# Softmax denominators added up on GpSimd instead of VectorE, in a two-block network of one core

## The chip, the core and the metric

The kernel runs on one core of one Trainium2 chip. The metric is device time in microseconds (us) of one execution. The core's engines each run their own queue of instructions in order: TensorE (PE in the rows; PEld is its weight load), VectorE (DVE), ScalarE (ACT), GpSimd (POOL) and SyncE (SP), which here issues all DMAs. Engines wait for each other through semaphores.

## What is computed

The network is a block with two hybrid layers (retention, neighbourhood attention and grouped-query attention in parallel, merged by gates), followed by a second block of feed-forward layers and two mixers. 256 tokens, a context of 256 more, width 1024, all in float32. The change touches the softmax of the two attentions. Cut to that:

```python
def attend(q, k, v):
    s = jnp.einsum('btkgd,bskd->bkgts', q, k).astype(jnp.float32) * (q.shape[-1] ** -0.5)
    p = jax.nn.softmax(s, axis=-1)
    return jnp.einsum('bkgts,bskd->btkgd', p, v)
...
        s_all = jnp.concatenate([s.reshape(s.shape[:5] + (n_loc,)), s_ctx], axis=-1)
        p = jax.nn.softmax(s_all, axis=-1)
        p_loc = p[..., :n_loc].reshape(s.shape)
        p_ctx = p[..., n_loc:]
        return jnp.einsum('bhrjqwk,brwjkhd->brjqhd', p_loc, vb) + jnp.einsum('bhrjql,blhd->brjqhd', p_ctx, vc)
...
    for layer in range(DEPTH):
        x, y = hybrid_layer(x, y, ..., need_ctx=layer < DEPTH - 1)
```

Layer 0 gives results for the 256 tokens and for the context (512 queries); layer 1 for the tokens alone (256 queries).

## The kernel before

Everything is kept transposed: the 128 partitions hold keys (or channels), the free dimension holds queries. A product is made in several fp32r passes of a high and a low part (`mm3`, `split`, `pair`), so a weight is first cast to a high part by ScalarE (`wh`) and its rest is subtracted by VectorE (`wl`).

One call of `scores` handles one head. Its scores lie in tiles of 128 keys: `s_loc` holds the scores against the two token tiles side by side, `cs` those against the two context tiles (two tiles of 512 queries in layer 0, one tile with both halves in layer 1). Then, in this order of the data: VectorE takes the maximum over the key tiles into `m`; GpSimd's `partition_all_reduce` takes the maximum of `m` over the 128 partitions and leaves it in all of them (`mx`, line 801); VectorE subtracts `mx` from every score tile; ScalarE takes the exponential (line 815); `pair` splits it into high and low parts; TensorE multiplies them with the values (`av`). For the denominator, VectorE adds the tiles of exponentials over the key tiles into `d` (lines 820 to 825: one add of the two context tiles, and one for each token tile), and a second `partition_all_reduce` sums `d` over the partitions (`den`, line 826). `den` is not needed by `av`; `pair_sums` (line 866) needs it, once both heads of a pair are multiplied, and the pair's result `o` is needed by the merge of its branch (`t_merge`).

The adds are there where `both` is set: in the four head pairs of neighbourhood attention of layer 0 (tiles named L0n), the four pairs of grouped-query attention of layer 0 (L0g) and the four pairs of neighbourhood attention of layer 1 (L1n). That is 24 calls of `scores` and 72 adds. Grouped-query attention of layer 1 (L1g) gets its denominators from TensorE. In neighbourhood attention a token key tile reaches only 160 of the 256 token queries (`REACH`), so the two adds of `s_loc` are 128x160; in L0g they are 128x256; the first add is 128x512 in layer 0 and 128x256 in layer 1.

The program does not write its instructions in the order in which they run. Every call goes to a recorder (`_Recorder.record`, which issues all of them from line 343, so nearly every row carries that line); `schedule` then plays the whole program through a list scheduler, with a cost for each operation from `cost` and a due time, and `issue` writes each engine's instructions in the planned order. So the costs in `cost` set the order on every engine. TensorE's queue mixes the attention of one branch with the merge of another: the L0m rows are merge products, L0gk keys and values, `ada_ps` modulation.

Of the kernel before, what the change touches and what calls it, by code (L numbers as in the profile page):

```python
# [10 lines left out]
ALU = mybir.AluOpType  # L11
# [4 lines left out]
T = 256  # L16
# [87 lines left out]
class _Recorder:  # L104
# [19 lines left out]
    def cost(self, eng, method, out, ins, kw):  # L124
        n = 1
        for e in out.shape[1:]:
            n *= e
        psum = any(i.space == bass.MemoryType.PSUM for i in ins) or out.space == bass.MemoryType.PSUM
        if eng == "tensor":
            rhs = ins[-1]  # L130
            n = 1
            for e in rhs.shape[1:]:
                n *= e
            d = max(n, 64) / 2400.0 * (4 if rhs.dtype == F32 and method == "matmul" else 1) + 0.002
            return d * 0.31 if out.shape[0] == 32 else d
        if eng == "scalar":
            return (n + (61 if psum else 112)) / 1200.0 + 0.093 * (len(ins) - 1)
        if eng == "vector":
            per = {"reciprocal": 6.0, "tensor_tensor_scan": 2.0}.get(method, 1.0)
            if method == "tensor_scalar" and not psum:  # L140
                per = 0.5
            if method == "tensor_reduce":
                n = 1
                for e in ins[0].shape[1:]:
                    n *= e
            return (66 + per * n) / 960.0 + (0.06 if method == "scalar_tensor_tensor" and len(ins) == 3 else 0)
        if eng == "gpsimd":
            return 0.38 + 7.5 * n / 1200.0 if method == "partition_all_reduce" else 0.09 + n / 1200.0
        b = 4
        for e in out.shape:  # L150
            b *= e
        return b / 360e3
# [193 lines left out]
class _K:  # L346
# [410 lines left out]
    def scores(self, qk, nq, bias, scale, both):  # L757

        nc = self.nc

        def passes(out, ks, n):
            for i, (k, q) in enumerate(qk):
                self.mm(out, lhsT=k[:, ks], rhs=q[:, n], start=i == 0, stop=i == len(qk) - 1)

        v2 = self.v2
        sx = self.ps()
        reach, w = (FULL, T) if bias is None else (REACH, NR)  # L770
        for kt in range(2):
            passes(sx[:, w * kt : w * kt + w], slice(P * kt, P * kt + P), reach[kt])
        cs = []
        m = self.f()
        if nq == T:
            s = self.ps()
            for kt in range(2):
                ks = slice(T + P * kt, T + P * kt + P)
                passes(s[:, 256 * kt : 256 * kt + 256], ks, FULL[0])
            c = self.f()  # L780
            nc.scalar.copy(c, s)
            self.tt(m[:, :T], c[:, :T], c[:, T:], ALU.max)
            cs.append(c)
        else:
            for kt in range(2):
                s = self.ps()
                ks = slice(T + P * kt, T + P * kt + P)
                passes(s, ks, slice(0, nq))
                c = self.f()
                nc.scalar.copy(c, s)  # L790
                cs.append(c)
            self.tt(m, cs[0], cs[1], ALU.max)
        s_loc = self.f()
        if bias is None:
            nc.scalar.copy(s_loc, sx)
        else:
            self.tt(s_loc[:, : 2 * w], sx[:, : 2 * w], bias, ALU.add)
        for kt, c in enumerate(reach):
            self.tt(m[:, c], m[:, c], s_loc[:, w * kt : w * kt + w], ALU.max)
        mx = self.f()  # L800
        nc.gpsimd.partition_all_reduce(mx[:, :nq], m[:, :nq], channels=P, reduce_op=RED.max)
        mb = mx[:, :T].unsqueeze(1).to_broadcast([P, 2, T])
        out = []
        for i, e in enumerate([s_loc] + cs):
            n = 2 * w if i == 0 else T2
            if i == 0 and bias is not None:
                ml = mx[:, :T]
                ml = bass.AP(ml.tensor, ml.offset, [list(ml.ap[0]), [T - NR, 2], [1, NR]])
                ev = e[:, :n].rearrange("p (a b) -> p a b", a=2)
                self.tt(ev, ev, ml, ALU.subtract)  # L810
            elif i == 0 or nq == T:
                self.tt(v2(e), v2(e), mb, ALU.subtract)
            else:
                self.tt(e, e, mx, ALU.subtract)
            self.act(e[:, :n], e[:, :n], AF.Exp, scale=scale)
            out.append(self.pair(e, n))
        if not both:
            return out, None
        den, d = self.f(), self.f()
        if nq == T:  # L820
            self.tt(d[:, :T], cs[0][:, :T], cs[0][:, T:], ALU.add)
        else:
            self.tt(d, cs[0], cs[1], ALU.add)
        for kt, c in enumerate(reach):
            self.tt(d[:, c], d[:, c], s_loc[:, w * kt : w * kt + w], ALU.add)
        nc.gpsimd.partition_all_reduce(den[:, :nq], d[:, :nq], channels=P, reduce_op=RED.add)
        return out, den

# [412 lines left out]
    def v2(self, t):  # L1241
        return t.rearrange("p (a b) -> p a b", a=2)
# [446 lines left out]
```

## Time and profile before

| | |
|---|---|
| median of 3 runs | 1872.78 us (1872.41 to 1873.35) |
| the profiled execution's own time | 1871.89 us |
| its span in the trace | 1870.1 us |
| TensorE busy | 1831.5 us (98%), 11392 matmuls |
| VectorE busy | 1489.0 us (80%) |
| ScalarE busy | 1108.9 us (59%) |
| GpSimd busy | 206.7 us (11%), 152 instructions |
| share of TensorE in the chain that ended last | 90% |

The span leaves out 1.8 us around the program. A busy share is an average over the whole program; attention of layer 0 lies between about 160 and 500 us of the span, neighbourhood attention of layer 1 between about 780 and 890 us. A row of the trace gives a start, a duration and, in brackets, how long the engine sat idle before it and which instruction ended that.

### The profile page before, as it was taken

The page shows a single profiled execution, that of the slowest core. Times are in us where ns is not written, and L with a number is a line of the kernel's source. Part 1 is how long each engine was busy: PE and PEld are TensorE (multiplying, and loading weights), DVE is VectorE, ACT ScalarE, POOL GpSimd, SP SyncE. Part 2 cuts the span into 40 slices and gives each one's busy share as a digit, 9 for nine tenths or more (in the row PEclk, how much of TensorE's full clock was granted, in tenths as well). Part 3 has the DMA queues.
Part 4 walks back from the last instruction along what each step waited for, and adds up shares of the span by engine and source line. Part 5 has one row for each costly group of instructions (what it writes and reads, how often), then busy time and mean ns, then how long its engine had stood idle before and what let it go on. Part 6 is the DMA issues. An engine that isn't in the chain of part 4 may idle for free.

```text
span 1870.1 us, 29383 instructions
## 1 busy us (share of the span) xinstructions
PE 1831.5 (98%) x11392; PEld 1618.8 (87%) x11392; DVE 1489.0 (80%) x2389; ACT 1108.9 (59%) x1884; POOL 206.7 (11%) x152
## 2 busy tenths in 40 slices
PE   6999999999999999999999999999999999999998
PEld 4888787777889989999998889988888888988887
DVE  7778978699947699998789877898767876788764
ACT  4655555666545596766566556875546554756543
POOL 0133422042200021232000000000000010000000
PEclk9999999999999999999999999999999999999999
DMA  9432353334344323435656566265555555545552
GB/s 314 134 97 87 113 160 113 113 90 153 99 154 125 90 69 90 143 109 150 194 169 225 180 199 218 78 217 196 192 189 187 192 186 197 192 158 181 186 195 92
DMA packets 336235, 291.17 MB, mean 156 GB/s; under 512 B 9184, under 2 KB 325728, under 8 KB 336096
## 3 DMA queue, kind: packets, MB, share of 16 engines
q1 hardware_dynamic: 336096, 289.30, 49.0%
q8 instruction: 89, 1.46, 0.3%
q14 instruction: 50, 0.41, 0.1%
HBM read 288.22 MB, written 1.05 MB: 155 GB/s over the span
## 4 chain that ended last, share of the span: by engine, by line
PE 90%; DVE 6%; ACT 2%; issue 1%; DMA 0%; POOL 0%; SPq 0%; DVEq 0%; POOLq 0%; ACTq 0%
PE fb_ps L343 13%; PE L0m_ps L343 8%; PE f_ps L343 7%; PE fa_ps L343 7%; PE L1m_ps L343 5%; PE L0n_ps L343 5%; PE L1n_ps L343 4%; PE L0r_ps L343 4%; PE L1r_ps L343 4%; PE fb1b_ps L343 3%; PE f0b_ps L343 3%; PE fb0b_ps L343 3%; PE fa1b_ps L343 3%; PE mix_ps L343 3%; PE L0g_ps L343 3%; PE L0out_ps L343 3%
## 5 line engine op out<-in xcount | busy, mean ns | idle before, releaser
L343 PE MATMUL fb_ps<-fb_r,fb_wh 128*128 128x512 f32 x704 | 176.6, 393 | 0.0
L343 PEld LDWEIGHTS fb_ps<-fb_r,fb_wh 128*128 128x128 f32 x704 | 126.7, 189 | 22.8
L343 ACT CAST fb_wh<-fb_raw 128x1024 fp32r<-128x1024 f32 x88 | 92.1, 1049 | 87.1 <-PE fb_ps L343 58.3
L343 DVE TENSOR_TENSOR fb_wl<-fb_raw,fb_wh 128x1024 fp32r<-128x1024 f32 x88 | 107.6, 1223 | 35.7 <-ACT fb_wh L343 35.4
L343 PE MATMUL L0m_ps<-L0in_r,L0m_wh 128*128 128x512 f32 x384 | 121.2, 394 | 0.0
L343 PEld LDWEIGHTS fb_ps<-fb_r,fb_wl 128*128 128x128 f32 x704 | 96.0, 190 | 6.8
L343 PE MATMUL fb_ps<-fb_r,fb_wl 128*128 128x256 f32 x704 | 98.1, 282 | 0.0
L343 PE MATMUL f_ps<-f_r,f_wh 128*128 128x512 f32 x352 | 88.7, 393 | 0.0
L343 PE MATMUL fa_ps<-fa_r,fa_wh 128*128 128x512 f32 x352 | 88.4, 393 | 0.0
L343 PEld LDWEIGHTS L0m_ps<-L0in_r,L0m_wh 128*128 128x128 f32 x384 | 72.3, 190 | 16.4 <-issue 0.8
L343 POOL MEMSET mix_r<- 128x128 f32 (+1 forms) x36 | 7.4, 238 | 640.9 <-DVE fa_r L343 457.9
L343 DVE TENSOR_TENSOR L0g_r<-L0g_r,L0g_r 128x512 f32<-128x512 f32 (+3 forms) x116 | 71.5, 663 | 6.4 <-ACT L0g_r L343 3.8
L343 PE MATMUL L0m_ps<-L0in_r,L0m_wl 128*128 128x512 f32 x192 | 75.3, 393 | 0.0
L343 ACT ACT_TABLE_LOAD x56 | 71.8, 1283 | 4.4 <-PE L0out_ps L343 1.4
L343 ACT CAST fa_wh<-fa_raw 128x1024 fp32r<-128x1024 f32 x44 | 46.1, 1049 | 47.5 <-PE fa_ps L343 29.9
L343 PEld LDWEIGHTS fa_ps<-fa_r,fa_wh 128*128 128x128 f32 x352 | 63.4, 189 | 11.4
L343 PEld LDWEIGHTS f_ps<-f_r,f_wh 128*128 128x128 f32 x352 | 63.4, 189 | 11.4
L343 DVE TENSOR_TENSOR fa_wl<-fa_raw,fa_wh 128x1024 fp32r<-128x1024 f32 x44 | 53.8, 1223 | 24.3 <-ACT fa_wh L343 18.0
L343 PE MATMUL L1m_ps<-L0out_r,L1m_wh 128*128 128x256 f32 x384 | 71.9, 283 | 0.0
L343 ACT CAST f_wh<-f_raw 128x1024 fp32r<-128x1024 f32 x44 | 46.1, 1049 | 42.4 <-PE f_ps L343 24.6
L343 DVE TENSOR_TENSOR fb_r<-fb_r,fb_r 128x512 f32<-128x512 f32 (+2 forms) x132 | 65.7, 509 | 2.3 <-ACT fb_r L343 1.3
L343 ACT CAST L0m_wh<-L0m_raw 128x1024 fp32r<-128x1024 f32 (+1 forms) x48 | 40.1, 837 | 44.3 <-PE L0m_ps L343 25.9
(509 smaller groups left out, 5464.8 us busy)
## 6 DMA issues: line engine op xcount, KB each, us to landing
fb_raw<-in_ffn_w_in_dram SPq DMA_DIRECT2D x44, 1024.0 KB, 5.4
f_raw<-in_ffn_w_in_dram SPq DMA_DIRECT2D x22, 1024.0 KB, 5.2
fa_raw<-in_ffn_w_in_dram SPq DMA_DIRECT2D x22, 1024.0 KB, 5.2
ada_raw<-in_ada_w_dram SPq DMA_DIRECT2D x32, 512.0 KB, 4.8
L0m_raw<-in_w_in_dram SPq DMA_DIRECT2D x24, 512.0 KB, 3.8
L1m_raw<-in_w_in_dram SPq DMA_DIRECT2D x24, 512.0 KB, 4.2
L0in_raw<-in_ada_w_dram SPq DMA_DIRECT2D x32, 256.0 KB, 6.0
f0b_raw<-in_ffn_w_out_dram SPq DMA_DIRECT2D x8, 1024.0 KB, 5.5
```

What stands on the lines that cost most here:

```text
L343: getattr(getattr(self.real, eng), method)(*a, **k)
```

## The change

The three adds of the denominator are issued to GpSimd (the argument `nc.gpsimd` of `tt`) and not to VectorE. The maxima, the subtractions and both `partition_all_reduce` stay where they were. The planner's cost for GpSimd changes with it: an operation other than `partition_all_reduce` was 0.09 + n/1200 us for n elements a partition, and is now 0.1 us plus n/960 for each input (half of that for a memset, which has none). Since the planner sets the order, instructions move on the other engines too.

```diff
         if eng == "gpsimd":
-            return 0.38 + 7.5 * n / 1200.0 if method == "partition_all_reduce" else 0.09 + n / 1200.0
+            if method == "partition_all_reduce":
+                return 0.38 + 7.5 * n / 1200.0
+            return 0.1 + n * (len(ins) or 0.5) / 960.0
...
         if nq == T:
-            self.tt(d[:, :T], cs[0][:, :T], cs[0][:, T:], ALU.add)
+            self.tt(d[:, :T], cs[0][:, :T], cs[0][:, T:], ALU.add, nc.gpsimd)
         else:
-            self.tt(d, cs[0], cs[1], ALU.add)
+            self.tt(d, cs[0], cs[1], ALU.add, nc.gpsimd)
         for kt, c in enumerate(reach):
-            self.tt(d[:, c], d[:, c], s_loc[:, w * kt : w * kt + w], ALU.add)
+            self.tt(d[:, c], d[:, c], s_loc[:, w * kt : w * kt + w], ALU.add, nc.gpsimd)
         nc.gpsimd.partition_all_reduce(den[:, :nq], d[:, :nq], channels=P, reduce_op=RED.add)
```

VectorE's queue has 72 instructions fewer. GpSimd's has the 72 adds more, and 58 others that stand nowhere in the source: an `ISA` row without a tile is what the compiled program calls a reload of the engine's library, and the builder puts one wherever an add follows a `partition_all_reduce` or the other way round. Memsets need none. The program before has one such reload, ahead of its first `partition_all_reduce`; the changed one has 59: 20 of the new ones among the L0n heads, 20 among L0g, 18 among L1n.

GpSimd's queue of the kernel before, at the first two head pairs of L0n (an `ISA` row with tiles is a `partition_all_reduce`; 385 and 409 are the maxima of pair 0, 392 and 416 its denominators, 437 and 456 the maxima of pair 1):

```order
L343 ISA L0n_r_385<-L0n_r_379 128x512
L343 ISA L0n_r_409<-L0n_r_403 128x512
L343 MEMSET L0n_r_517 64x512
L343 ISA L0n_r_392<-L0n_r_393 128x512
L343 MEMSET L0n_r_518 64x512
L343 ISA L0n_r_416<-L0n_r_417 128x512
L343 ISA L0n_r_437<-L0n_r_431 128x512
L343 ISA L0n_r_456<-L0n_r_450 128x512
```

The same place of the changed kernel, from behind maximum 409 on:

```order
L345 ISA
L345 TENSOR_TENSOR L0n_r_393<-L0n_r_381,L0n_r_383 128x512
L345 MEMSET L0n_r_517 64x512
L345 TENSOR_TENSOR L0n_r_393<-L0n_r_393,L0n_r_384 128x160 x2
L345 ISA
L345 ISA L0n_r_392<-L0n_r_393 128x512
L345 ISA
L345 TENSOR_TENSOR L0n_r_417<-L0n_r_405,L0n_r_407 128x512
L345 MEMSET L0n_r_518 64x512
L345 TENSOR_TENSOR L0n_r_417<-L0n_r_417,L0n_r_408 128x160
L345 ISA
L345 ISA L0n_r_437<-L0n_r_431 128x512
```

Ahead of maximum 437 there now stand four reloads, five adds and one denominator (416 comes later); behind it, ahead of maximum 456, come two more reloads and one add.

GpSimd's queue of the kernel before at the last pair of L0g (948 and 970 are its maxima, 955 and 977 its denominators; behind it follow memsets of layer 1):

```order
L343 ISA L0g_r_948<-L0g_r_942 128x512
L343 ISA L0g_r_970<-L0g_r_964 128x512
L343 ISA L0g_r_955<-L0g_r_956 128x512
L343 ISA L0g_r_977<-L0g_r_978 128x512
L343 MEMSET L1gk_r_1305 128x2x64
```

And of the changed kernel:

```order
L345 ISA L0g_r_948<-L0g_r_942 128x512
L345 ISA L0g_r_970<-L0g_r_964 128x512
L345 ISA
L345 TENSOR_TENSOR L0g_r_956<-L0g_r_944,L0g_r_946 128x512
L345 TENSOR_TENSOR L0g_r_956<-L0g_r_956,L0g_r_947 128x256 x2
L345 ISA
L345 ISA L0g_r_955<-L0g_r_956 128x512
L345 ISA
L345 TENSOR_TENSOR L0g_r_978<-L0g_r_966,L0g_r_968 128x512
L345 TENSOR_TENSOR L0g_r_978<-L0g_r_978,L0g_r_969 128x256 x2
L345 ISA
L345 ISA L0g_r_977<-L0g_r_978 128x512
```

Four reloads and six adds now stand between the last maximum and the last denominator.

## Rows read from the trace of the kernel before

**Rows 1.** The page: span, engines' busy us, engines' shares of the chain that ended last.

```profile
span 1870.1 us, 29383 instructions
...
PE 1831.5 (98%) x11392; PEld 1618.8 (87%) x11392; DVE 1489.0 (80%) x2389; ACT 1108.9 (59%) x1884; POOL 206.7 (11%) x152
...
PE 90%; DVE 6%; ACT 2%; issue 1%; DMA 0%; POOL 0%; SPq 0%; DVEq 0%; POOLq 0%; ACTq 0%
```

**Rows 2.** Waits of TensorE: us in total, times, longest.

```profile
PE L0g_ps L343 <- DVE L0g_r L343: 2.5, 3, 1.5
PE L0n_ps L343 <- ACT L0n_r L343: 2.4, 1, 2.4
PE L0g_ps L343 <- ACT L0g_r L343: 1.9, 2, 1.4
```

**Rows 3.** VectorE's groups, 160 to 330 us: busy us, mean ns.

```profile
L343 DVE TENSOR_TENSOR L0n_r<-L0n_r,L0n_r 128x512 f32<-128x512 f32 x36 | 29.6, 840 | 0.7 <-ACT L0n_r L343 0.7
...
L343 DVE TENSOR_TENSOR L0n_r<-L0n_r,L0n_r 128x160 f32<-128x160 f32 x32 | 11.8, 371 | 0.3
```

**Rows 4.** VectorE's groups, 780 to 890 us, the same columns.

```profile
L343 DVE TENSOR_TENSOR L1n_r<-L1n_r 128x256 f32<-128x256 f32 x16 | 6.9, 438 | 0.3 <-ACT L1n_r L343 0.2
```

**Rows 5.** GpSimd's instructions from line 343: duration ns min/median/max, first and last start.

```profile
L343 POOL MEMSET L0n_r<- x8: 518/522/547, 100.6 to 224.3; 64x512 f32 x8
...
L343 POOLq MODIFY_POOL_CONFIG  x2: 11/11/11, 0.8 to 0.8; - x2
```

**Rows 6.** GpSimd's timeline, 330 to 520 us: start, us, what, idle before.

```profile
357.25 1.78 POOL L343 PARTITION_ALL_REDUCE L0g_r<-L0g_r  x1 [28.73 <-DVE L0g_r L343]
...
485.05 9.20 POOL L343 PARTITION_ALL_REDUCE L0g_r<-L0g_r  x2 [6.08 <-DVE L0g_r L343]
```

**Rows 7.** ScalarE's loads of function tables, in the page: busy us, mean ns.

```profile
L343 ACT ACT_TABLE_LOAD x56 | 71.8, 1283 | 4.4 <-PE L0out_ps L343 1.4
```

**Rows 8.** DMA issues: times, KB of each, median us from issue to landing.

```profile
fb_raw<-in_ffn_w_in_dram SPq DMA_DIRECT2D x44, 1024.0 KB, 5.4
...
L0r_raw<-in_w_in_dram SPq DMA_DIRECT2D x2, 1024.0 KB, 7.5
...
L0n_b<-in_na_dram SPq DMA_DIRECT2D x8, 160.0 KB, 3.4
```

**Rows 9.** GpSimd's timeline, 170 to 330 us.

```profile
178.43 2.08 POOL L343 PARTITION_ALL_REDUCE L0n_r<-L0n_r  x1 [3.92 <-DVE L0n_r L343]
...
191.61 5.28 POOL L343 PARTITION_ALL_REDUCE L0n_r<-L0n_r  x2 [5.10 <-DVE L0n_r L343]
198.77 2.08 POOL L343 PARTITION_ALL_REDUCE L0n_r<-L0n_r  x1 [1.88 <-DVE L0n_r L343]
...
303.14 3.23 POOL L343 PARTITION_ALL_REDUCE L0n_r<-L0n_r  x1 [1.77 <-DVE L0n_r L343]
```

**Rows 10.** TensorE's timeline, 205 to 214 us: products with the values, pair 1 of L0n.

```profile
205.24 0.50 PE L343 MATMUL L0n_ps<-L0n_r,L0n_r 128*128 128x512 f32 x1 [2.44 <-ACT L0n_r L343]
...
212.65 1.48 PE L343 MATMUL L0n_ps<-L0n_r,L0n_r 128*128 128x512 f32 x8
```

**Rows 11.** TensorE's timeline, 489 to 505 us: first wait of the merge of L0g.

```profile
504.63 0.50 PE L343 MATMUL L0m_ps<-L0g_r,L0m_wh 128*128 128x512 f32 x1 [0.77 <-DVE L0g_r L343]
```

**Rows 12.** GpSimd's timeline, 745 to 900 us: first and last of L1n.

```profile
791.51 1.06 POOL L343 PARTITION_ALL_REDUCE L1n_r<-L1n_r  x1 [19.44 <-DVE L1n_r L343]
...
884.51 3.58 POOL L343 PARTITION_ALL_REDUCE L1n_r<-L1n_r  x2 [10.08 <-DVE L1n_r L343]
```

**Rows 13.** TensorE's timeline, 908 to 911 us: the merge's first product with L1n.

```profile
909.48 0.40 PE L343 MATMUL L1m_ps<-L1n_r,L1m_wh 128*128 128x256 f32 x2
```

**Rows 14.** Stretch, length, busy us (instructions) by engine, granted clock, DMA share, GB/s.

```profile
378.71:385.54 6.83, 6.04 (x15) 4.62 (x16) 6.83 (x11) 5.42 (x10) 4.61 (x2) 0.50 0.52 144
...
200.00:210.00 10.00, 7.37 (x34) 5.52 (x33) 10.00 (x14) 6.96 (x13) 0.85 (x1) 1.00 0.66 186
```

**Rows 15.** VectorE's timeline, 170 to 210 us: an add beside a reduction.

```profile
191.99 2.04 DVE L343 TENSOR_TENSOR L0n_r<-L0n_r,L0n_r 128x160 f32<-128x160 f32 x1
```

## The prediction

> **What bounds the kernel now.** I read the page first, then the waits of TensorE, then the timelines of GpSimd and TensorE beside each other in the three stages where the moved adds stand. TensorE is busy 1831.5 of 1870.1 us and makes 90% of the chain that ended last [rows 1]: matmuls are the bound nearly everywhere, and the time can fall only by what TensorE waits. In the two attention stages of layer 0 these waits are 2.5 + 2.4 + 1.9 us, and 0.8 us more at the merge behind them [rows 2, 11]: 7.6 us, of which 3.3 us were ended by VectorE. After the short waits in L0g the granted clock was 0.50 of full speed for 6.83 us (the lower of the two levels, 1.2 GHz), which costs 3.4 us; around the single wait of 2.44 us in L0n it stayed 1.00 [rows 10, 14]. So relief of VectorE is worth at most 7.6 + 3.4 = 11 us. There is far more room the other way: TensorE's queue is in order, and a product with the values that waits for its exponentials holds up all that follows it.
>
> **What the change removes.** 72 adds leave VectorE. By its groups a 128x512 add takes 0.84 us, a 128x160 one 0.37, a 128x256 one 0.44 [rows 3, 4]. L0n: 8 heads x (0.84 + 2 x 0.37) = 12.6 us; L0g: 8 x (0.84 + 2 x 0.44) = 13.8; L1n: 8 x (0.44 + 2 x 0.37) = 9.4. That is 36 us of VectorE's time, but nearly all of it lies beside busy TensorE. I credit the 3.3 us of waits that VectorE ended.
>
> **What it adds to GpSimd: the adds.** No row shows an add on GpSimd. From below, a memset of 512 elements, which reads nothing, takes 0.52 us [rows 5]; from above, an undisturbed reduction over the partitions of 512 elements takes 1.78 us [rows 6]. I take the middle, 1.15 us, since an add reads two tiles but crosses no partitions, and in proportion 0.6 us for 256 and 0.4 us for 160 elements.
>
> **What it adds to GpSimd: the reloads.** The queue now holds 58 reloads of the engine's library, between adds and reductions. The one of before is two records of 11 ns at 0.8 us of the span, 85 us ahead of the first reduction [rows 5], so the trace doesn't show how long the engine can't work after one. The bounds: from below those records, or 1.28 us, what ScalarE takes to load a table of functions [rows 7]; from above 7.5 us, the slowest landing of a DMA in the rows, 1 MB; a piece of 160 KB lands after 3.4 us, the most frequent load of 1 MB after 5.4 us [rows 8]. A reload is a program that is fetched while the engine stands still, so I put it with the transfers and take **R = 5.4 us**.
>
> The Trainium skill, GPSIMD Engine Reference, section 2.1, speaks against this change: the first call of a freshly loaded kernel "additionally pays an IRAM-load of approximately 6 µs", with no instruction in the profile that shows it. No run here shows that yet; the records of 11 ns agree with its being invisible. With 6 us the sum below would come to about 2010 us, an estimate from that page.
>
> **Where the reloads lie: L0n.** The second maximum of pair 0 ends at 180.5 us and that of pair 1 at 200.85 [rows 9]. Between them the changed queue has six reloads; the six adds of pair 0, 2 x (1.15 + 0.4 + 0.4) = 3.9 us; two memsets, 1.0; one denominator, 3.2 [rows 9]; two maxima at 2.1, 4.2. That is 12.3 + 6R = 44.7 us, so the maximum ends at 225.2 us, 24.4 us late. The first head's product stood waiting when it began 8.35 us after its maximum (191.61 + 5.28 to 205.24); the second head's began 11.8 us after its own, at 212.65 [rows 9, 10], so 3.4 us are slack. TensorE waits **21 us** more there. In pairs 2 and 3 GpSimd catches up in its idle time before it, and I take 3 us (0 to 6) for the last maximum.
>
> **L0g.** Here GpSimd has no rest. Its work from the first maximum on: 8 maxima at 2.1 and 8 denominators at 3.2 us, 42.4; adds 8 x (1.15 + 1.2) = 18.8; four memsets, 2.1; 20R = 108. Together 171.3 us. The same stretch took 357.25 to 494.25 = 137.0 us [rows 6]. 10.4 us behind it TensorE already stood waiting for that result [rows 11], so there is no slack: **34.3 us**, partly at the products with the values, the rest at the merge.
>
> **L1n.** Eight maxima at 1.1 and eight denominators at 1.8 us, 23.2 [rows 12]; adds 8 x (0.6 + 0.8) = 11.2; memsets 0.6; 18R = 97.2. Together 132.2 us against 791.51 to 888.09 = 96.6 [rows 12]. The merge first uses the result at 909.48 [rows 13], 21.4 us later; if 10.4 us are needed, as in L0g, 11 are slack. **24.6 us**.
>
> **The rest of the change.** The planner moves some L0m matmuls past products of L0g and turns casts round on ScalarE; the work is the same, and it lies beside the waits above: nothing. If that cover were gone, a cast or product a place further back costs about its own length, half a microsecond. SyncE's order hardly changes. The waits come in about eight places, each longer than the ones that brought the clock down once, so I add 8 x 3.4 = 27 us for the clock (0 to 27).
>
> **The sum.** 21 + 3 + 34.3 + 24.6 = 82.9 us of waits, 27 us of clock, less 3.3: 1871.9 + 106.6 = 1978.5 us against the profiled execution's own time, which lies 0.9 us under the median of the runs shown: **1979 us**. With R = 3.4 only the first place in L0n is left, 9 us and one drop of the clock: 1882. With R = 7.5 the waits are 33.6 + 15.6 + 76.3 + 62.4 = 188 us: 2085. Adds at 0.52 or 1.78 us instead of 1.15 shift the waits by about 18 us either way.
>
> **Rivals.** *The reloads are nearly free, and VectorE's relief counts.* For it: the records last 11 ns, and a reload can run while GpSimd waits for exponentials anyway. The walk in L0n comes out even at R = (20.3 + 3.4 - 12.3) / 6 = 1.9 us, in L0g and L1n at 3.7 and 4.0; under 1.9 us nothing is late and between 0 and 11 us of waits and clock go: 1862 to 1873, 1866 where it is the larger part. Against it: 1.28 us is the only row as low as that, and it is another engine's. *The reloads are nearly free, but the adds hold VectorE up.* A 128x160 add beside a reduction took 2.04 us, and its group's mean is 0.37 [rows 3, 15]: an instruction of VectorE that reads two tiles waits for GpSimd. If each of the 72 adds (0.8 us on average) holds VectorE for half its length, 29 of the 36 us come back and the time stays: 1872, up to 1880 if they fall on the critical subtractions. The Trainium skill, SBUF — State Buffer, section Who interferes with whom, has this as a rule: the two share a read port, and the later one is fully blocked; the row agrees. *The reloads cost more than 7.5 us*, since they fetch beside the weights' transfers: each further microsecond is worth about 50 us, so 2100 and more.
>
> **How the numbers follow.** Forecast (R from 3.4 to 7.5 us, slower): 0.71. Dearer reloads: 0.08, slower. Cheap reloads with a gain: 0.12, of which 0.10 by more than 0.2% and 0.02 within. Cheap reloads with the adds in VectorE's way: 0.09, of which 0.06 within and 0.03 slower. Together faster 0.10, same 0.08, slower 0.82; 0.2% (3.7 us) is about what a measurement of this kernel tells from no change. The range reaches from the cheap end, 1864, to 2085; beyond it I leave the dear reloads and the larger gains.
>
> **What would show it.** Right: behind a maximum GpSimd starts its add, and behind an add its reduction, some 5 us late with no engine to wait for; TensorE waits 15 us or more for ScalarE or VectorE at pair 1 of L0n; the stretch from the first maximum of L0g to its last denominator grows from 137 to 170 us or more, that of L1n from 97 to 130; low granted clocks follow the waits; GpSimd appears in the chain; from 950 us of the old span on nothing but the shift changes. Wrong: adds that follow a maximum by less than 2 us, with TensorE's waits as before; then a rival holds. Adds far above 1.8 us would shift the blame from the reloads to the adds.

## The result, and the profile after

The changed kernel takes 2173.11 us (median, 2170.65 to 2173.89) against 1872.6 us in the same comparison: 1.160 times as long (95% interval 1.159 to 1.162). That is 300.5 us more, where I had forecast 106 more and 2085 us as the upper end. The direction was right, the size far out.

The page of the changed kernel: span, busy times, and the shares of the chain that ended last.

```profile
span 2168.8 us, 29522 instructions
...
PE 1866.5 (86%) x11392; PEld 1642.3 (76%) x11392; DVE 1456.0 (67%) x2317; ACT 1108.6 (51%) x1884; POOL 251.8 (12%) x224
...
PE 73%; issue 12%; POOL 5%; DVE 4%; ACT 3%; DMA 1%; SPq 0%; POOLq 0%; DVEq 0%; ACTq 0%
```

Against [rows 1], TensorE is busy 35 us longer and idle some 264 us longer; "issue" has gone from 1% to 12% of the chain. An engine that waits "for issue" has nothing to wait for that the trace shows. Which engine that is, the timeline of GpSimd shows from the first maxima of L0n on (start, us, what, idle before it and what ended that):

```profile
177.48 2.08 POOL L345 PARTITION_ALL_REDUCE L0n_r<-L0n_r  x1 [3.91 <-DVE L0n_r L345]
186.40 1.61 POOL L345 TENSOR_TENSOR L0n_r<-L0n_r,L0n_r 128x512 f32<-128x512 f32 x1 [6.84 <-ACT L0n_r L345]
188.07 0.52 POOL L345 MEMSET L0n_r<- 64x512 f32 x1
188.67 1.28 POOL L345 TENSOR_TENSOR L0n_r<-L0n_r,L0n_r 128x160 f32<-128x160 f32 x2
195.85 3.25 POOL L345 PARTITION_ALL_REDUCE L0n_r<-L0n_r  x1 [5.90 <-issue]
206.61 1.25 POOL L345 TENSOR_TENSOR L0n_r<-L0n_r,L0n_r 128x512 f32<-128x512 f32 x1 [7.50 <-issue]
207.81 0.52 POOL L345 MEMSET L0n_r<- 64x512 f32 x1
208.30 0.51 POOL L345 TENSOR_TENSOR L0n_r<-L0n_r,L0n_r 128x160 f32<-128x160 f32 x1
214.75 1.80 POOL L345 PARTITION_ALL_REDUCE L0n_r<-L0n_r  x1 [5.94 <-issue]
223.56 0.51 POOL L345 TENSOR_TENSOR L0n_r<-L0n_r,L0n_r 128x160 f32<-128x160 f32 x1 [7.00 <-issue]
229.79 5.05 POOL L345 PARTITION_ALL_REDUCE L0n_r<-L0n_r  x2 [5.73 <-issue]
```

This is the library reload, visible only as a gap: in these rows 5.7 to 5.9 us ahead of a reduction, 6.8 to 7.5 us ahead of an add that follows one (in the whole trace up to 7.4 and 7.6), and nothing where an add or a memset follows an add. The gap of 6.84 us that is put down to ScalarE is by its length of the same kind. The adds are short: 1.25 us for 512 elements and 0.51 for 160 where nothing disturbs them.

The waits of TensorE of the changed kernel (us in total, times, longest) answer to [rows 2], which came to 7.6 us with the merge:

```profile
PE L1n_ps L345 <- ACT L1n_r L345: 53.6, 2, 29.4
PE L0n_ps L345 <- ACT L0n_r L345: 41.8, 4, 20.3
PE L0g_ps L345 <- ACT L0g_r L345: 37.3, 4, 21.5
PE L0g_ps L345 <- ACT L0m_r L345: 27.4, 1, 27.4
PE L0m_ps L345 <- ACT L0g_r L345: 23.5, 1, 23.5
PE L0gk_ps L345 <- ACT L0gk_r L345: 22.9, 1, 22.9
PE L0n_ps L345 <- DVE L0n_r L345: 18.4, 3, 14.5
PE L1m_ps L345 <- ACT L1m_wh L345: 18.0, 1, 18.0
```

Nearly all of them end on ScalarE, and three of the names have nothing to do with a maximum: L0gk, L0m and the weight casts L1m_wh. What ScalarE itself waited for is in its own waits, the three rows that name GpSimd:

```profile
ACT L1n_r L345 <- POOL L1n_r L345: 100.5, 4, 27.0
ACT L0g_r L345 <- POOL L0g_r L345: 93.3, 4, 30.9
ACT L0n_r L345 <- POOL L0n_r L345: 72.8, 4, 30.9
```

Twelve waits, 266.6 us. One is of 1.88 us; the other eleven, 11.2 to 30.9 us each and 264.7 together, stand before the same instruction, the copy of the second head's denominator in `pair_sums`, in eleven of the twelve head pairs. Before the change ScalarE waited for GpSimd at the same tiles as well, but only for 22.4 us:

```profile
ACT L0n_r L343 <- POOL L0n_r L343: 12.3, 4, 5.9
ACT L0g_r L343 <- POOL L0g_r L343: 5.7, 3, 2.1
ACT L1n_r L343 <- POOL L1n_r L343: 4.4, 2, 2.9
```

ScalarE's timeline of the changed kernel shows one of the eleven with what was queued behind it:

```profile
411.98 0.61 ACT L345 COPY L0n_r<-L0n_r 64x512 f32<-64x512 f32 x1 [30.88 <-POOL L0n_r L345]
412.62 1.28 ACT L345 ACT_TABLE_LOAD   x1
413.91 0.69 ACT L345 ACTIVATE L0gk_r<-L0gk_ps,eps 128x512 f32<-128x512 f32 x1
414.50 0.58 ACT L345 COPY L0gk_r<-L0gk_ps 128x512 f32<-128x512 f32 x1
414.96 0.63 ACT L345 CAST L0m_wh<-L0m_raw 128x512 fp32r<-128x512 f32 x1
```

and TensorE's timeline shows who stood still for that:

```profile
415.13 0.69 PE L345 MATMUL L0gk_ps<-cstt,L0gk_r 128*128 128x128 f32 x2 [22.94 <-ACT L0gk_r L345]
```

The copy waits 30.88 us for the last denominator of L0n. Behind it in the same in-order queue stand an activation and a copy of the next stage (L0gk), whose inputs need no denominator, and a weight cast. VectorE sat idle for 30.47 us ahead of its reciprocal, behind the same copy. TensorE waits 22.94 us for the L0gk copy. The denominators are read late in the program's logic, but early in the planner's order, which takes GpSimd to have none of these gaps.

At pair 1 of L0n, where the forecast had put its first wait, TensorE's timeline shows two:

```profile
219.11 1.52 PE L345 MATMUL L0n_ps<-L0n_r,L0n_r 128*128 128x512 f32 x2 [17.27 <-ACT L0n_r L345]
...
236.18 1.57 PE L345 MATMUL L0n_ps<-L0n_r,L0n_r 128*128 128x512 f32 x5 [14.46 <-DVE L0n_r L345]
```

The clock fell with the waits. The stretch around TensorE's two waits at pair 1 of L0n and the one around the wait above, with the columns of [rows 14]:

```profile
206.70:240.80 34.10, 6.93 (x16) 4.71 (x17) 11.89 (x16) 10.23 (x18) 9.47 (x7) 0.50 0.06 16
394.40:425.10 30.70, 4.57 (x12) 3.40 (x13) 11.82 (x12) 7.82 (x11) 7.10 (x7) 0.50 0.00 0
```

TensorE worked only 6.93 and 4.57 us in them, so half the clock (1.2 GHz) costs only a part of these few us; over the whole program the clock's cost is at most about the 35 us by which TensorE's busy time grew.

### The profile page after: what moved, and what is told of

Its sections match the earlier page's. It is cut to its first block, busy times and chain, and to the rows that moved or that the text cites. A ratio compares the mean times of both kernels' runs of the same rounds, so it can differ in the third digit from the quotient of the medians.

```text
span 2168.8 us, 29522 instructions
## 1 busy us (share of the span) xinstructions
PE 1866.5 (86%) x11392; PEld 1642.3 (76%) x11392; DVE 1456.0 (67%) x2317; ACT 1108.6 (51%) x1884; POOL 251.8 (12%) x224
## 4 chain that ended last, share of the span: by engine, by line
PE 73%; issue 12%; POOL 5%; DVE 4%; ACT 3%; DMA 1%; SPq 0%; POOLq 0%; DVEq 0%; ACTq 0%
PE fb_ps L345 11%; PE L0m_ps L345 7%; PE f_ps L345 6%; PE fa_ps L345 6%; PE L1m_ps L345 4%; PE L1r_ps L345 4%; PE L0r_ps L345 3%; PE L0n_ps L345 3%; PE fb1b_ps L345 3%; PE f0b_ps L345 3%; PE fb0b_ps L345 3%; PE fa1b_ps L345 3%; PE mix_ps L345 2%; PE L1n_ps L345 2%; PE L0out_ps L345 2%
## 5 line engine op out<-in xcount | busy, mean ns | idle before, releaser
L345 PEld LDWEIGHTS fb_ps<-fb_r,fb_wh 128*128 128x128 f32 x704 | 126.7, 189 | 22.8
L345 DVE RECIPROCAL L0g_r<-L0g_r 128x512 f32<-128x512 f32 x8 | 26.8, 3351 | 90.0 <-ACT L0g_r L345 90.0
L345 PE MATMUL L0n_ps<-L0n_r,L0n_r 128*128 128x512 f32 (+1 forms) x128 | 29.3, 373 | 60.1 <-ACT L0n_r L345 41.8
L345 DVE TENSOR_TENSOR L0g_r<-L0g_r,L0g_r 128x512 f32<-128x512 f32 (+3 forms) x92 | 60.9, 701 | 29.9 <-POOL L0g_r L345 22.6
L345 DVE TENSOR_TENSOR L0n_r<-L0n_r,L0n_r 128x512 f32<-128x512 f32 (+4 forms) x80 | 49.1, 650 | 47.1 <-POOL L0n_r L345 44.0
L345 PEld LDWEIGHTS L0n_ps<-L0n_r,L0n_r 128*128 128x128 f32 x128 | 22.4, 210 | 66.6 <-ACT L0n_r L345 43.5
```

The costliest lines, as they stand in the source:

```text
L345: getattr(getattr(self.real, eng), method)(*a, **k)
```

## Experiments

Two theories were left after this. **Early readers**: the gaps make GpSimd late, and what costs the time is that readers of the denominators stand early in ScalarE's queue and block what is behind them. **Late maxima**: the forecast's own mechanism, a chain on GpSimd that holds up the maxima. The rivals were the adds themselves beside VectorE, and the planner's changed price. In the expectations, theory 1 is the switches with early readers, theory 2 is the adds or their reading beside VectorE, and the forecast's theory is late maxima; a switch is a change between adds and reductions on GpSimd, which brings a reload. All runs but one edit the changed kernel. A run's ratio, with the 95% interval in brackets, is to the kernel before, measured beside it.

### The switches without the large adds

```diff
-            self.tt(d, cs[0], cs[1], ALU.add, nc.gpsimd)
+            self.tt(d, cs[0], cs[1], ALU.add)
...
+        self.tt(d[:, :1], d[:, :1], self.zero, ALU.add, nc.gpsimd)
         nc.gpsimd.partition_all_reduce(den[:, :nq], d[:, :nq], channels=P, reduce_op=RED.add)
```

> The 72 large adds of the denominators are back on VectorE; ahead of each of the 24 denominator reductions GpSimd makes one 128x1 add of a column of zeros. This keeps the switches of GpSimd's code and takes its large adds away: 48 of the 58 switches that the changed kernel has over the one before. Theory 1 (the switches make GpSimd late, at 6.5 us each by the gaps of the profile after, and ScalarE's wait for the denominators blocks what is queued behind it): most of the 300 us stays, 48/58 of it or 248 us, so about 2120 us (2060 to 2180), with waits of 10 to 30 us of ScalarE for GpSimd at the head pairs. Theory 2 (the large adds themselves, or GpSimd and VectorE reading side by side): little is left, 1890 us or less. The forecast's theory (GpSimd's own chain holds up the maxima, and the denominators matter only at the merge): between the two, 1873 + 48 x 1.8 (106 us over 58 switches) = 1960 us.

Measured: 2081.95 us, ratio 1.113 (1.111 to 1.115). 24 adds of one column cost 211 us with 48 switches, 4.4 us each. ScalarE's waits for GpSimd are there again, 246.7 us:

```profile
ACT L0n_r L345 <- POOL L0n_r L345: 95.2, 4, 28.9
ACT L1n_r L345 <- POOL L1n_r L345: 76.7, 4, 23.3
ACT L0g_r L345 <- POOL L0g_r L345: 74.8, 4, 22.4
```

So the switches cause 211 of the 300 us without the large adds on GpSimd. The time lies a little under the share by count (2120).

### The adds' work without the switches

```diff
-            self.tt(d, cs[0], cs[1], ALU.add, nc.gpsimd)
+            for e in (cs[0], m):
+                nc.gpsimd.tensor_copy(d, e)
...
```

> Each of GpSimd's adds is replaced by two copies of the same size on GpSimd, so that GpSimd still reads as many bytes at the same places and VectorE is still without the 72 adds, while GpSimd's code need not be switched between them and the reductions; what is left out is the sum over the key tiles, so the denominators are not the reference's. Theory 1: nearly all of the 300 us is gone; 1860 to 1890 us, and the run shows what relieving VectorE is worth by itself. Theory 2 (GpSimd's data work, or its reading beside VectorE): a large part stays, over 1950 us. The forecast's theory, without the switches: 1870 to 1890 us.

Measured: 1878.46 us, ratio 1.004 (1.002 to 1.005). With 144 copies on GpSimd and one load of its library, as before, 7.5 us of the 300 are left. A copy of 512 elements took 0.83 us there in the mean of L0n and 0.93 in that of L0g.

### Nobody reads the denominators

```diff
-        return out, den
+        return out, mx
```

> The changed kernel, with all its adds, reductions and switches, but the outputs are divided by the maxima, and nobody reads the denominators: their wait on ScalarE is taken away, the division itself stays. Theory 1: ScalarE's 12 waits for GpSimd, 267 us in the profile after, are gone, and only late maxima are left, so 1930 to 1990 us. The forecast's theory (late maxima and GpSimd's chain set the time): stays near the changed kernel, over 2100 us, as the maxima still come out of the same chain on GpSimd. Theory 2: also over 2100 us.

Measured: 1998.73 us, ratio 1.068 (1.067 to 1.070). The reading of the denominators is worth 174 us, and 126 us stay: 9 us more than the upper edge of what early readers alone were to leave. ScalarE's waits for GpSimd in the three stages were expected to be gone; they are down to 55.2 us, and 40 of them stand at the same copy, which here waits for a maximum. What the rest is, the stretch from the first maximum of L0g to its last denominator shows, 394.0 to 605.1 us (length, then busy us and instructions of PE, PEld, DVE, ACT, POOL, then clock, DMA share, GB/s):

```profile
394.00:605.10 211.10, 173.65 (x793) 132.60 (x792) 150.37 (x180) 98.69 (x156) 68.29 (x43) 0.89 0.30 91
```

GpSimd is busy 68.3 us of 211.1. 20 switches lie in this stretch, and the 142.8 us that are left make 7.1 us for each. 6.9 us of it are the gap itself; 4.1 us of the stretch are waits for VectorE that no switch covers. The same sum gives 7.1 for L0n (208.4 us, 8.7 of them such waits) and 7.0 for L1n (169.6 us, 18 switches, 2.8 us). GpSimd has next to no free time in any of the three stretches, although the page gives it 13% of the span. Before the change they took 143.0, 137.0 and 96.6 us. This is the forecast's mechanism, and it is worth 126 us, not 300.

### A planner that knows the switches

```diff
-        table = None
+        table = lib = None
...
+                    if e == "gpsimd" and op.call[1] in ("tensor_tensor", "partition_all_reduce"):
+                        start += 0 if op.call[1] == lib else 6.5
+                        lib = op.call[1]
                     end = at[e] = start + op.dur
```

> The changed kernel, with a planner that adds 6.5 us to an instruction of GpSimd whenever it goes from adds to reductions or back. In its order the switches fall from 59 to 31, and the readers of the denominators are planned later. Theory 1: both the number of switches and ScalarE's blocked queue shrink, so 1950 to 2060 us, with the waits of ScalarE for GpSimd under half of the 267 us. If GpSimd's own throughput sets the time, 30 switches at 6.5 us still stand in the attention: 1873 + 300 x 30/58 = 2028 us with the waits of ScalarE per switch as before. Theory 2: the adds are all still there, over 2100 us.

Measured: 1895.71 us, ratio 1.014 (1.012 to 1.015). All 72 adds are on GpSimd, 30 added switches remain, and 24.7 us are left of 300. In ScalarE's waits GpSimd is named only once more, with 1.1 us in the retention of layer 1. It fell below every expectation: 30 switches that are known in the plan cost 0.8 us each, against 5.2 in the changed kernel. But the run changes two things, the number of switches and the place of the readers. The runs after it take them apart.

### The planner's price alone

This run edits the kernel before: the adds are on VectorE, and only the changed price of an instruction on GpSimd in the planner is taken over.

> All adds are on VectorE as in the kernel before; only the planner's price for an instruction on GpSimd is the changed kernel's. The order on the queues may move, the work does not. Theory 1, and the forecast's term of zero for the planner's price: 1866 to 1878 us, as before. A theory that the changed price made a bad order and thereby a share of the 300 us: over 1890 us.

Measured: 1871.51 us, ratio 1.000 (0.999 to 1.001). The price alone does nothing.

### Only layer 1

```diff
-            self.tt(d, cs[0], cs[1], ALU.add, nc.gpsimd)
+            self.tt(d, cs[0], cs[1], ALU.add, nc.gpsimd if nq == T else None)
...
```

> GpSimd makes the adds in layer 1 alone (24 of the 72 adds, 8 of the 24 heads, 18 of the 58 added switches), VectorE in layer 0. If the cost sits where the switches are, stage by stage, the time lost is the one that layer 1 lost in the changed kernel: its attention took 193.7 us there against 96.6 before, 97 us more, so about 1968 us (1940 to 1985), and the L1n waits of TensorE stay as they were. A forecast by shares of the switches gives 1873 + 300 x 18/58 = 1966 us, no other. If the three attention stages make each other late, it is clearly under 1940 us.

Measured: 1972.86 us, ratio 1.054 (1.052 to 1.056). The cost sits where the switches are, a third of it in layer 1, and the stages don't make each other late: L1n's stretch takes 200.6 us here, 193.7 in the changed kernel. TensorE's two longest waits there are the ones of the changed kernel:

```profile
PE L1n_ps L345 <- ACT L1n_r L345: 55.4, 2, 32.0
PE L1m_ps L345 <- ACT L1m_wh L345: 17.6, 1, 17.6
```

### The same switches, the readers placed later

```diff
-                heapq.heappush(events, (end, 1, i))
+                late = 30.0 if op.call[3].get("reduce_op") == RED.add else 0.0
+                heapq.heappush(events, (end + late, 1, i))
```

> The changed kernel, whose planner takes each denominator to arrive 30 us after GpSimd's reduction has ended, while GpSimd is taken as free at that end as before. So the readers of the denominators (copy on ScalarE, reciprocal on VectorE) are placed later in their queues, and GpSimd still changes its code 55 times (59 in the changed kernel), which the planner still does not price. Theory 1 (the queue behind the early-placed readers is what is lost): falls to where nobody reads the denominators, 1999 us, or a little under it (1950 to 2010), and ScalarE's waits for GpSimd on denominators are nearly gone. If the switches by their number or GpSimd's own lateness cost the time, it stays over 2100 us.

Measured: 2000.61 us, ratio 1.069 (1.068 to 1.071). With 55 of the 59 switches, and the denominators read, only later, it lands 2 us from the run in which nobody reads them. ScalarE's waits for GpSimd shrink from 266.6 us to 5.1:

```profile
ACT L0n_r L346 <- POOL L0n_r L346: 2.2, 2, 1.7
ACT L1n_r L346 <- POOL L1n_r L346: 2.1, 1, 2.1
ACT L0g_r L346 <- POOL L0g_r L346: 0.8, 1, 0.8
```

So the 172 to 174 us are the place of the readers in the queue, not their work and not the number of switches. And the 126 to 129 us that stay are not ScalarE's waits for GpSimd, which are as good as gone here.

### Maxima placed later as well

```diff
-                heapq.heappush(events, (end, 1, i))
+                late = 25.0 if op.call[1] == "partition_all_reduce" else 0.0
+                heapq.heappush(events, (end + late, 1, i))
```

> As the run whose planner takes the denominators 30 us late, but with 25 us and for the maxima as well: the exponentials that wait for a maximum are placed later too. GpSimd still changes its code 53 times, unpriced. Theory 1, extended: what is left when nobody waits early for denominators (126 us over before) is the same mistake of order on the maxima, so this run falls well under 1999 us, to 1880 to 1930 us, although nearly all switches are there. If late maxima cost that rest whatever the order, as the forecast had it (83 us and the clock), it stays at 1960 us or more.

Measured: 2033.18 us, ratio 1.087 (1.085 to 1.089). My extension fell: with 52 added switches in the attention this order doesn't take the rest away, and it became larger. The run doesn't show that no order could. 25 us were also no longer enough for the denominators, and ScalarE's waits for GpSimd are back at 121.3 us: ScalarE waits 32.5 us for the last one of L0g and 22.8 us for the last one of L1n.

### As many switches as in the changed kernel, all in the plan

The planner with the price, and one add of a column of zeros on GpSimd ahead of each maximum too.

```diff
+        if both:
+            self.tt(m[:, :1], m[:, :1], self.zero, ALU.add, nc.gpsimd)
         nc.gpsimd.partition_all_reduce(mx[:, :nq], m[:, :nq], channels=P, reduce_op=RED.max)
```

> The run whose planner prices each switch of GpSimd's code at 6.5 us, with all large adds on GpSimd, and one 128x1 add of zeros on GpSimd ahead of each of the 24 maxima as well. This brings the switches from 31 to 61, about the changed kernel's 59, all of them now in the plan. If the plan alone decides (a known lateness costs next to nothing), it stays near the run with 31, 1896 to 1930 us. If the number of switches has a price of its own because GpSimd then has no time left in the attention (60 x 6.5 us = 390 us of switching beside about 377 us that the three attention stages took before), it goes to where 54 to 58 switches stood with the denominators out of the way, 1980 to 2080 us.

Measured: 2019.11 us, ratio 1.079 (1.077 to 1.081). From 31 to 61 planned switches the time goes from 1896 to 2019 us, 4.1 us for each of the 30. The stretch of L0g is full again:

```profile
408.10:620.20 212.10, 152.32 (x649) 111.77 (x647) 119.92 (x143) 79.33 (x126) 73.39 (x50) 0.86 0.25 76
```

73.4 us busy and 20 switches at 6.9 us make its 212.1. With 10 switches in it, in the run with 31, the stretch was 167.0 us, and GpSimd still waited there for TensorE, VectorE and ScalarE. So a known switch costs little while GpSimd has time left, and much once it has none. The added switches come with the adds directly ahead of the maxima, so this run alone doesn't part their number from their place. That L0g's stretch is as long as the 211.1 us of the run with as many unknown switches speaks for the number.

### The priced plan, with the large adds on VectorE

The first run (a column of zeros before each denominator) with the planner of the fourth.

> The run with the switches alone (all 72 large adds on VectorE, one 128x1 add on GpSimd per denominator; 2082 us with 48 added switches unpriced), with the planner that prices a switch at 6.5 us; the switches fall to 33. If large adds on GpSimd cost nothing by themselves, this lands where the run with them and 31 switches lies, 1885 to 1910 us. If they have a price of their own, it is under 1885 us. If the priced plan had helped the other run only by way of VectorE's relief, it stays over 1950 us.

Measured: 1885.02 us, ratio 1.007 (1.005 to 1.009), at the edge between two expectations. 32 known switches cost 13 us, and the 72 large adds on GpSimd, with two switches fewer and VectorE relieved of them, come to some 11 us more (1895.71): a small price, but a price, in another order.

### No adds at all

```diff
-        den, d = self.f(), self.f()
-        if nq == T:
...
+        den, d = self.f(), cs[0]
         nc.gpsimd.partition_all_reduce(den[:, :nq], d[:, :nq], channels=P, reduce_op=RED.add)
-        return out, den
+        return out, mx
```

> The 72 adds are left out on both engines and no switch of GpSimd's code is added: each reduction of a denominator goes over one key tile, and the outputs are divided by the maxima. This is the most that taking the adds off VectorE can bring, whoever makes them. The forecast credited 3.3 us, at most 11 (7.6 us of TensorE's waits and what goes with them): 1862 to 1872 us. If VectorE held the attention more than its waits show, under 1860 us.

Measured: 1877.91 us, ratio 1.003 (1.002 to 1.005): 6 us slower than with the adds on VectorE, outside both expectations. In the order that this planner makes there is no prize in taking the adds off VectorE, whoever makes the sums. VectorE's busy time fell by 19.5 us (1489.0 to 1469.5), not by the 36 that the adds took, since other instructions of it grew longer. One of VectorE's groups in L0n (busy us, mean ns) in this run

```profile
L345 DVE TENSOR_TENSOR L0n_r<-L0n_r,L0n_r 128x512 fp32r<-128x512 f32 x20 | 17.8, 896 | 2.2 <-ACT L0n_r L345 2.0
```

and before:

```profile
L343 DVE TENSOR_TENSOR L0n_r<-L0n_r,L0n_r 128x512 fp32r<-128x512 f32 x20 | 13.4, 682 | 0.0
```

682 has become 896 ns, with GpSimd doing nothing but the reductions of before. The two engines' timelines, laid beside each other, show where: 17 of the 20 took 0.68 to 0.69 us, and the other three, which began while a reduction was running, took 1.82, 2.20 and 2.31 us, until some 0.4 us before its end. Where the 6 us come from, a different order of the planner's or those longer instructions, stays open too: TensorE's waits on VectorE in L0n and L0g are 4.8 and 7.2 us, against 0.2 and 2.5.

## Why the prediction was right in direction and wrong in size

- **The bound, and the relief.** TensorE as the bound held. The 3.3 us that I credited for VectorE's relief are not there: without any adds the time is 6 us worse. The 36 us that I counted for the adds are too many, since I took group means: in the first run, where GpSimd is seldom beside it, the group of 0.84 us has a mean of 0.68.
- **The adds.** I took 1.15, 0.6 and 0.4 us; undisturbed ones took 1.25, 0.71 and 0.51. Their groups' means are higher beside VectorE's work, up to 1.82 us for 512 elements in L0g. The 72 cost some 11 us of time where the plan knows the switches.
- **The reload.** I took 5.4 us from the loads of 1 MB, with 3.4 and 7.5 as bounds. The gaps are 5.7 to 7.6 us, some 6.5 in the mean (104.3 us in 16 gaps of L0g), as good as within the bounds and above the value taken. That a load of 1 MB comes near them is luck: no run ties the two together. With 6.5 in the forecast's own working the waits come to 27.6 + 3 + 56.3 + 44.4 = 131 us, with the clock and the credit 155, some 2027 us. The Trainium skill, GPSIMD Engine Reference, section 2.1, has about 6 us for the load of a kernel's code that its first call pays. The gaps of 5.7 to 5.9 us ahead of a reduction agree; those ahead of an add are longer.
- **L0n, pair 1.** I forecast 21 us of waits; TensorE waited 17.27 us before its first product there and 14.46 before its second. The place was right, the size short, and the first head was late as well.
- **L0g and L1n.** I forecast stretches of 171.3 and 132.2 us. With no readers in the way they take 211.1 and 169.6, with them 241.6 and 193.7. The planner moves other work into the longer stretches (173.65 us of TensorE's in the L0g one, which was 137.0 us long in all before), so the 212 us that the three grow make 126 us of time. That this lies so near the 106 us I forecast is partly luck: the stretches grew far more than I had them grow, and less of it counted.
- **The clock.** I took 27 us; TensorE's busy time grew by 35.
- **The step that failed** is the path from GpSimd to TensorE. I let a late GpSimd reach TensorE at two places only, "at the products with the values, the rest at the merge", and of all that the planner moves elsewhere, casts on ScalarE included, I wrote "the work is the same, and it lies beside the waits above: nothing". I took the denominators to be needed at the merge only, and looked at what TensorE needs from GpSimd. I didn't ask what is queued behind the copy on ScalarE that waits for a denominator, in an order made by a planner that has no price for a reload. That is a missing term of 172 to 174 us, more than all the others together: 300 is 126 to 129 for a GpSimd without free time, which was forecast at 106, and this. The planner's changed price by itself did cost nothing (1871.51 us).
- **The signs.** All the signs that I had named for "right" came, and most were larger than named. The run in which nobody reads the denominators shows them as well, so they couldn't tell the forecast's mechanism from one with a further term.
- **The rivals.** *Dearer reloads* gave the size nearly, for a wrong reason: no reload lay above 7.5 us by much. *Cheap reloads with the adds in VectorE's way* was worked out at 1872 to 1880 us, and that is what the run without switches shows, 1878.5. (The 0.8 us that I wrote for an average add is 0.63 by my own lengths, which gives 23 us back and not 29; the runs' own mean is 0.97.) VectorE's busy time was 1487.1 us in it and 1488.7 in the first run with the priced plan, against 1469.5 without any adds: about half of the 36 us is given back beside GpSimd's work. The Trainium skill, SBUF — State Buffer, section Who interferes with whom, has the rule that a VectorE instruction with two inputs and a GpSimd instruction that reads contend for a shared read port, and that the later one is blocked. The three long instructions of the run without adds agree with that. In time the difference between the two runs without switches is 0.6 us.

## What to carry to other kernels

Before work goes to an engine that runs loaded code, count how often its queue would go from one kind of operation to another, and multiply: 58 switches at some 7 us are 400 us, which is free only where the engine idles that long, and the engine's busy share doesn't show it. A result that comes late costs not where it is used but where its first reader stands in an in-order queue, so list what stands behind each reader on its own engine. When a planner sets the order, give it the cost before judging the move: the same 72 adds cost 300 us unpriced and 25 priced, the plan having halved the switches as well. Even so they were not worth moving here.

## What the runs showed of the hardware that I had not expected

- A switch between adds and reductions on GpSimd takes 5.7 to 5.9 us towards a reduction and 6.8 to 7.5 us towards an add in the rows shown of L0n (5.7 to 7.6 in the whole trace), each time again; the records that mark it, two for each, last 12 ns in the median, and only the gap shows it. Memsets and copies need none: with 144 copies among the reductions there was one load.
- GpSimd's adds take longer than its copies: for 512 elements the shortest add took 1.25 us and the shortest copy 0.61, the groups' means are 1.37 to 1.82 and 0.83 to 0.93.
- Taking 36 us of two-tile adds off VectorE shortened its busy time by 19.5 us where nobody made them, by 1.9 where GpSimd made copies of the same sizes, and by 33.0 in the changed kernel. With the adds back on VectorE and 48 switches it was 1462.8 us, less than without any adds. So its busy time depends on how many of its instructions fall into one of GpSimd's, and not only on how many it has.
